# Turning twelve blocks of rows by the DMA, as two planes of 16-bit halves, in a decoder layer on one core

## The chip, the cores and the metric

The kernel runs on one core of a Trainium2 chip. The metric is the device time of one execution in microseconds (us), the median of several runs. Beside it stands one execution taken by the hardware profiler, with a record for nearly every instruction and every DMA.

The engines, as the profile names them: PE multiplies matrices (PEld loads its weights), DVE is the vector engine, ACT the scalar engine, POOL the general one, and SP issues most of the DMAs. A DMA issued by an engine stands in that engine's own queue, in order with its other instructions: the profile calls them SPq and ACTq.

## The reference

One decoder layer, batch 1, 256 tokens, width 2048, all in float32. The part that matters here, with the weights' names:

```python
merged = sigmoid(g_a) * (ret_out @ w_proj_ret) + sigmoid(g_b) * (rnn_out @ w_proj_rnn)
h = h + merged @ w_mix_out
hn = rmsnorm(h, norm_xa_w)
h = h + memory_cross_attention(hn, mem_n, xa_w_q, xa_w_k, xa_w_v, xa_w_o)
hn = rmsnorm(h, norm_ffn_w)
h = h + conv_gated_ffn(hn, ffn_w_up, ffn_conv_w, ffn_conv_b, ffn_w_down)
```

`ret_out` comes from an eight-head retention, `rnn_out` from a gated linear recurrence; both, and the gates, are projections of the normalised input by `w_in`. What counts for the change is that `merged` and the two later values of `h` are each a 256 x 2048 matrix that the kernel makes with tokens on the partitions, and that the next product needs with features on the partitions.

## The kernel before

**The products.** Every weight matrix is read once, in chunks of 512 x 512 (KC = 4 row tiles of 128, 1 MB each), in the order of a list `plan`. `prefetch` (L182) issues the chunk's load on SP into `raw` (three buffers), then splits it into a high part `hi`, rounded to fp32r (a cast on ACT, L214), and a low part `lo` = raw - hi (DVE, L215); there are six buffers of each, two for a chunk. The other operand is split likewise, so that a product is three matmuls: high by high, low by high, high by low.

`gemm_n` (L283) makes a block of 256 tokens x 512 columns with tokens on the partitions, in four chunks of 24 matmuls when the inner size is 2048. `gemm_t` (L246) makes the block with features on the partitions, in four chunks of 32 matmuls. Both take their chunks from `chunks` (L229). It splits two chunks ahead (AHEAD), counts the chunks in `step`, and after each chunk runs what is due in the list `pending`. `later(n, fn)` (L225) puts a piece of work there that is to be issued n + 1 chunks on. So the side work (turning, softmax, recurrence) stands between the matmuls of later chunks. A scheduler then orders each engine's instructions: of those that are ready, the one that was written first.

**The operand by feature.** The operand of a product is a list of tiles, each holding two feature tiles of 128 for all 256 tokens, high half in columns 0 to 255 and low half in 256 to 511. `split_pair` (L323, ACT L330 and DVE L331) makes one with a common factor, `split_cols` (L349, ACT L353 and DVE L354) one with a factor for each feature (the norm's weight).

**The turns.** `transposed` (L303) turns rows on PE: for each 256 columns of a 512-column block, four 128 x 128 transposes against an identity matrix (`ident`, in `cid`) into one PSUM tile `sm` (L309). Three places use it for blocks of 512 columns that DVE has just finished:

- merged rows: `gated` (L679) makes gate times product for a block b; for the second gate DVE finishes the block (L686) and adds the other branch's (L698). `turn_merged` (L691) turns it. Its four blocks (b = 0 to 3) feed the product with `w_mix_out`.
- residual rows after the mixers, and after the attention: `residual` (L707) runs `gemm_n` with `w_mix_out` or `xa_w_o`, adds the block to the residual rows `hrow[b]` (DVE, L714), has ACT square them for the norm (L730), and puts two calls of `turn` (L720) on the list, one chunk apart, 256 columns each. The four blocks after the mixers become `h1s`, first read by the product with `xa_w_q`, after one of four chunks with `xa_w_k`. Those after the attention become `h2s`, read by the first product with `ffn_w_up`, which follows at once.

The first chunk of the product that follows reads tiles 0 and 1 of its list, the fourth tiles 6 and 7. So the last block (b = 3) of the merged rows has three chunks from its product's end until it is read, and so has the last block of `h2s`.

**Buffers and loads.** The tiles called `big` are 4 KB per partition and come from a pool of 27. The residual's own rows (`x`) and the memory tokens are loaded on SP between the third and the fourth product stage (L703, L704: eight loads of 512 KB), and squares of the memory rows (`rms`, L429, 16 instructions of ACT over the whole kernel, eight of them here) follow in the product with `w_mix_out` at b = 1.

PE also turns the retention's heads (`finish_head`, 32 transposes) and the attention's probabilities (16, L783).

Of the kernel before, what the change touches and what calls it, by code (L numbers as in the profile page):

```python
# [9 lines left out]
F32 = mybir.dt.float32  # L10
F32R = mybir.dt.float32r
I32 = mybir.dt.int32
AF = mybir.ActivationFunctionType
ALU = mybir.AluOpType
AX = mybir.AxisListType

P = 128
D = 2048
S = 256
# [8 lines left out]
BW = 512  # L28
# [36 lines left out]
def hybrid_layer(  # L65
# [25 lines left out]
    act, dve, pe, pool, sp = nc.scalar, nc.vector, nc.tensor, nc.gpsimd, nc.sync  # L91
# [11 lines left out]
    def nm(s):  # L103
        count[0] += 1
        return f"{s}_{count[0]}"

    def big(shape, dt=F32, s="b"):
        return bp.tile(shape, dt, tag="big", name=nm(s))
# [4 lines left out]
    def acc():  # L113
        return pm.tile([P, 2, BW], F32, tag="acc", name=nm("acc"))

    def small(shape=(P, 2, S)):
        return px.tile(list(shape), F32, tag="sm", name=nm("sm"))
# [24 lines left out]
    early = sp_.tile([P, 1], F32, tag="pt3", bufs=2, name="early")  # L142
    act.activation(early, ones[:, 0:1], AF.Identity, scale=ones[:, 1:2])
    warm = px.tile([P, 2, S], F32, tag="sm", name="warm")
# [80 lines left out]
    def later(n, fn):  # L225

        pending.append((step[0] + n + 1, fn))

    def chunks(nk, w, row, c):  # L229

        w_, row_, nk_, c_ = plan[gemms[0]]
        assert (row_, nk_, c_) == (row, nk, c) and w_.tensor is w.tensor, (gemms[0], row, nk, c)
        gemms[0] += 1
        for k in range(0, nk, KC):
            prefetch(1)
            (r_, c_), parts = ahead.pop(0)
            assert (r_, c_) == (row + k * P, c)
            prefetch(AHEAD)
            yield k, parts
            step[0] += 1  # L240
            due = [p for p in pending if p[0] <= step[0]]
            pending[:] = [p for p in pending if p[0] > step[0]]
            for _, fn in due:
                fn()

    def gemm_t(w, row, st, nk, col):  # L246

        accs = [acc(), acc()]
        first = gemms[0] == 0
        phase = 0  # L250
        for k0, parts in chunks(nk, w, row, col):
            last = k0 + KC >= nk
            tiles = [(kk, j) for j in range(2) for kk in range(KC)]
            if first and k0 == 0:
                runs = [[(t, pr, kk, j) for t in (0, 1)] for pr in range(2) for kk in range(KC) for j in range(2)]
            elif last:
                runs = [[(t, pr, kk, j) for kk, j in tiles] for pr in range(2) for t in (1 - pr, pr)]
            else:
                runs = [[(t, pr, kk, j) for pr in range(2) for kk, j in tiles] for t in (phase, 1 - phase)]
                phase = 1 - phase  # L260
            for i, run in enumerate(runs):
                for t, pr, kk, j in run:
                    k = k0 + kk
                    sx = st[k // 2][:, k % 2, :]
                    part = parts[kk // KH][t][:, kk % KH, (2 * pr + j) * P : (2 * pr + j + 1) * P]
                    a = accs[pr][:, j, :]
                    if t == 1:
                        a, sx = a[:, S:BW], sx[:, 0:S]
                    pe.matmul(  # L269
                        a, part, sx, start=k == 0 and t == 0, stop=k == nk - 1 and t == 0, skip_group_check=True  # L270
                    )
                if i + 1 == len(runs) // 2 and not last:
                    st[(k0 + KC) // 2 + 1]
        return accs

# [27 lines left out]
    def transposed(rows):  # L303

        for k in range(0, rows.shape[2], 2 * P):
            t = small()
            for j in range(2):
                for tt in range(2):
                    pe.transpose(  # L309
                        t[:, j, tt * P : (tt + 1) * P], rows[:, tt, k + j * P : k + (j + 1) * P], ident  # L310
                    )
            yield t

    def joined(a, s="j"):

        c = tmp("c")
        o = tmp(s)
        with tc.high_priority(URGENT):
            act.copy(c, a[:, :, S:BW])  # L319
            dve.tensor_tensor(out=o, in0=a[:, :, 0:S], in1=c, op=ALU.add)  # L320
        return o

    def split_pair(src, scale=None):  # L323

        t = big([P, 2, BW], F32R, s="s")
        if scale is None:
            act.copy(t[:, :, 0:S], src)
            dve.tensor_tensor(out=t[:, :, S:BW], in0=src, in1=t[:, :, 0:S].bitcast(F32), op=ALU.subtract)
        else:
            act.mul(t[:, :, 0:S], src, scale)  # L330
            dve.scalar_tensor_tensor(  # L331
                out=t[:, :, S:BW], in0=src, scalar=scale, in1=t[:, :, 0:S].bitcast(F32),
                op0=ALU.mult, op1=ALU.subtract,
            )
        return t
# [13 lines left out]
    def split_cols(src, wcol):  # L349

        t = big([P, 2, BW], F32R, s="s")
        for j in range(2):
            act.activation(t[:, j, 0:S], src[:, j, :], AF.Identity, scale=wcol(j))  # L353
            dve.scalar_tensor_tensor(  # L354
                out=t[:, j, S:BW], in0=src[:, j, :], scalar=wcol(j), in1=t[:, j, 0:S].bitcast(F32),
                op0=ALU.mult, op1=ALU.subtract,
            )
        return t
# [60 lines left out]

    posi = big([P, S], I32, s="posi")  # L420
    sp.dma_start(out=posi, in_=positions[0].partition_broadcast(P))

    def rms(rows, pin=False):

        ss = sp_.tile([P, 2, 4], F32, tag="ss0", name=nm("ss"))
        for c in range(4):
            for tt in range(2):
                junk = tp.tile([P, BW], F32, tag="tmp", name=nm("junk"))
                i = act.activation(junk, rows[c][:, tt, :], AF.Square, accum_out=ss[:, tt, c : c + 1])  # L429
                if pin:  # L430
# [27 lines left out]
    def tables():  # L458
# [9 lines left out]
        dve.tensor_scalar(out=red, in0=red, scalar1=3.1415925, scalar2=-3.1415925, op0=ALU.min, op1=ALU.max)  # L468
        act.activation(sin, red, AF.Sin)
        dve.scalar_tensor_tensor(out=ang, in0=red, scalar=-1.0, in1=red, op0=ALU.mult, op1=ALU.max)  # L470
        dve.tensor_scalar(out=ang, in0=ang, scalar1=-1.0, scalar2=float(np.pi / 2), op0=ALU.mult, op1=ALU.add)
        act.activation(cos, ang, AF.Sin)
        dve.scalar_tensor_tensor(out=sin, in0=sin, scalar=sign, in1=rsb, op0=ALU.mult, op1=ALU.mult)
# [84 lines left out]
    for g in range(2):  # L558
        dec = big([P, 4, S], s="dec")
        vs, turned = [], []  # L560
        for b, o in enumerate((O_Q, O_K)):
            a = qjoin if g == b == 0 else [joined(t, "q") for t in gemm_t(w0, 0, xs, NT, o + g * BW)]
            if b == 0:
                sp.dma_start(
                    out=dec,
                    in_=consts[:, C_DEC + g * 4 * S : C_DEC + (g + 1) * 4 * S].rearrange("p (h s) -> p h s", s=S),
# [9 lines left out]
        for b in range(2):  # L576
            a = gemm_n(w0, 0, xs, NT, O_G + g * 1024 + b * BW)
            t = big([P, 2, BW], s="gate")
            for tt in range(2):
                act.activation(t[:, tt, :], a[:, tt, :], AF.Tanh, scale=half_rs0[:, tt : tt + 1])  # L580
            dve.scalar_tensor_tensor(out=t, in0=t, scalar=1.0, in1=a, op0=ALU.add, op1=ALU.mult)
# [67 lines left out]
    for b in range(4):  # L649
# [4 lines left out]
        for pr, a in enumerate(gemm_t(w0, 0, xs, NT, O_XR + b * BW)):  # L654
            z = scaled(a, "xz")
            for j in range(2):
                t = 4 * b + 2 * pr + j
                y = xr[:, 2 * pr + j, :]
                act.activation(y, z[:, j, :], AF.Identity, scale=p_cw(3, t), bias=p_cb(t))
                for s in range(1, 4):  # L660
                    dve.scalar_tensor_tensor(
                        out=y[:, s:S], in0=z[:, j, 0 : S - s], scalar=p_cw(3 - s, t), in1=y[:, s:S],
# [3 lines left out]
        for pr, a in enumerate(gemm_t(w0, 0, xs, NT, O_YR + b * BW)):  # L666
# [7 lines left out]
                out=gl[:, 2 * pr : 2 * pr + 2, :], in0=th, scalar=1.0, in1=y, op0=ALU.add, op1=ALU.mult  # L674
# [13 lines left out]

    merged = []

    def turn_merged(m, pr):  # L691
        for t in transposed(m[:, :, pr * S : (pr + 1) * S]):
            merged.append(split_pair(t, 0.5))

    mb = [gated(O_GB, w_proj_rnn[0], rnn, b, big([P, 2, BW], s="mb")) for b in range(4)]
    for b in range(4):
        m = gated(O_GA, w_proj_ret[0], ret, b, big([P, 2, BW], s="m"))
        dve.tensor_add(m, m, mb[b])  # L698
        for pr in range(2):
            later(pr, lambda m=m, pr=pr: turn_merged(m, pr))  # L700


    hrow = [load_rows(x, c) for c in range(4)]  # L703
# [3 lines left out]
    def residual(w, st, out, wcol, steps=None):  # L707

        ss = sp_.tile([P, 2, 4], F32, tag="ss0", name=nm("ss"))
        for b in range(4):  # L710
            if steps:
                steps(b)
            h = hrow[b]
            dve.tensor_add(h, h, gemm_n(w, 0, st, NT, b * BW))  # L714
            squares(h, ss, b)
            for pr in range(2):
                later(pr, lambda b=b, pr=pr: turn(b, pr, out, wcol))
        return ss

    def turn(b, pr, out, wcol):  # L720
        for t in transposed(hrow[b][:, :, pr * S : (pr + 1) * S]):
            out.append(split_cols(t, lambda j: wcol(4 * b + 2 * pr + j)))

    def squares(y, ss, i):
        for tt in range(2):
# [166 lines left out]
    for part, nb_ in enumerate(FF_PARTS):  # L892
# [13 lines left out]
        if final:  # L906
            wfin = []
            for i in range(2):
                t = big([P, 2, BW], s="wf")
                sp.dma_start(  # L910
                    out=t.rearrange("p a n -> p (a n)"),
                    in_=final_norm_w[i * 1024 : (i + 1) * 1024].partition_broadcast(P),
# [40 lines left out]
```

## Time and profile before

| | |
|---|---|
| runs shown | 2049.11, 2049.55, 2050.26 us; median 2049.55 |
| profiled execution, its own time | 2048.89 us |
| its span, first to last instruction | 2047.1 us |
| granted PE clock | 0.999 of full speed |
| PE, DVE, ACT busy | 2035.0, 1309.3, 1045.3 us |
| transposes of the three places | 96: 32 of `m`, 64 of `nat` |
| DMA | 392.25 MB, mean 192 GB/s |

A stage is found by the lines that work in it. In microseconds from the span's start: the second gate's four blocks end at about 836, the product with `w_mix_out` runs from there to about 923, the attention's four products fill the time to about 1220, the product with `xa_w_o` lies at about 1221 to 1308, and the feed-forward part from 1308 to the end.

How to read the profile's lines: "x64" counts instructions; "270/272/273" is the shortest, median and longest duration in ns; "out<-in" names the tiles that an instruction writes and reads; what stands behind a bar or in brackets is the idle time of the engine before the instruction, and what ended it. Matmuls overlap in PE's pipeline, so that a duration is longer than the step from one start to the next. The chain of waits follows back, from the last instruction, what released each piece of work, and gives each piece the time by which it moved the end.

### The profile page before, as it was taken

To read this page: it belongs to the slowest core of one execution; us is meant where nothing else is said; L and a number is where in the kernel's file an instruction comes from. 1 tells how busy PE (TensorE), PEld (TensorE's weight loads), DVE (VectorE), ACT (ScalarE), POOL (GpSimd) and SP (SyncE) were. 2 spreads that over 40 slices of the span, in tenths; PEclk is the share of its full clock that TensorE was granted. 3 is DMA by queue.
4 is the path that set the end of the run, shared out by engine and by line. 5 is a ranking of instruction groups with operands and counts; after the bars stand their busy time and mean duration, and the time that the engine had idled before them with its cause. 6 is when DMAs were issued, how large, how long until landed. Compare 5 with 4: busy or idle time off the path is not lost.

```text
span 2047.1 us, 26196 instructions
## 1 busy us (share of the span) xinstructions
PE 2035.0 (99%) x10508; PEld 1746.4 (85%) x10508; DVE 1309.3 (64%) x1630; ACT 1045.3 (51%) x1357; POOL 7.7 (0%) x12
## 2 busy tenths in 40 slices
PE   9999999999999999999999999999999999999998
PEld 7888888888888888888888888888888888888887
DVE  6858758888444544566555555577764777656774
ACT  6545447677434444555444544455543555435553
POOL 0000000000000000000000000000000000000000
PEclk9999999999999999999999999999999999999999
DMA  9664554555655555766555555555555555655563
GB/s 327 210 211 152 199 191 160 175 178 180 209 187 196 192 185 190 261 210 211 176 178 176 174 173 176 179 180 198 193 185 205 184 188 185 202 189 182 189 216 114
DMA packets 200682, 392.25 MB, mean 192 GB/s; under 512 B 7024, under 2 KB 11760, under 8 KB 200560
## 3 DMA queue, kind: packets, MB, share of 16 engines
q1 hardware_dynamic: 199040, 387.95, 55.7%
q10 hardware_dynamic: 1520, 2.63, 0.4%
q8 instruction: 82, 1.34, 0.3%
q14 instruction: 40, 0.33, 0.0%
HBM read 388.46 MB, written 2.10 MB: 191 GB/s over the span
## 4 chain that ended last, share of the span: by engine, by line
PE 79%; DVE 0%; ACT 0%; issue 0%; POOLq 0%; DVEq 0%
PE acc L269 35%; PE acc L280 14%; PE acc L281 14%; PE acc L279 14%; PE sm L297 1%; PE sm L309 1%; PE sm L623 0%; DVE xr L640 0%; PE sm L783 0%; ACT hi L214 0%; ACT nat L878 0%; DVE lo L215 0%; ACT c L319 0%; PE sm L380 0%; ACT s L330 0%
## 5 line engine op out<-in xcount | busy, mean ns | idle before, releaser
L215 DVE TENSOR_TENSOR lo<-raw,hi 128x1024 fp32r<-128x1024 f32 (+1 forms) x713 | 860.3, 1222 | 608.4 <-ACT hi L214 562.4
L214 ACT CAST hi<-raw 128x1024 fp32r<-128x1024 f32 x711 | 736.2, 1052 | 718.3 <-PE acc L280 455.0
L269 PE MATMUL acc<-s,hi 128*128 128x512 f32 x2688 | 639.0, 391 | 2.5 <-ACT hi L214 1.9
L279 PE MATMUL acc<-hi,s 128*128 128x512 f32 (+1 forms) x1528 | 591.9, 387 | 0.0
L281 PE MATMUL acc<-lo,s 128*128 128x512 f32 (+1 forms) x1528 | 590.1, 386 | 0.0
L280 PE MATMUL acc<-hi,s 128*128 128x512 f32 (+1 forms) x1528 | 590.0, 386 | 0.0
L269 PEld LDWEIGHTS acc<-s,hi 128*128 128x128 f32 x2688 | 496.5, 188 | 101.7 <-ACT hi L214 2.7
L269 PEld LDWEIGHTS acc<-s,lo 128*128 128x128 f32 x2688 | 342.7, 191 | 11.8 <-DVE lo L215 1.1
L269 PE MATMUL acc<-s,lo 128*128 128x256 f32 x2688 | 350.4, 283 | 0.5 <-DVE lo L215 0.5
L281 PEld LDWEIGHTS acc<-lo,s 128*128 128x128 f32 x1528 | 287.1, 188 | 57.9
L280 PEld LDWEIGHTS acc<-hi,s 128*128 128x128 f32 x1528 | 287.2, 188 | 57.1 <-DVE s L331 0.4
L279 PEld LDWEIGHTS acc<-hi,s 128*128 128x128 f32 x1528 | 287.2, 188 | 56.6
L319 ACT COPY c<-acc 128x512 f32<-128x512 f32 x84 | 48.6, 581 | 111.8 <-PE acc L269 111.8
L320 DVE TENSOR_TENSOR uz<-acc,c 128x512 f32<-128x512 f32 x44 | 30.3, 688 | 27.4 <-ACT c L319 27.4
L835 DVE SCALAR_TENSOR_TENSOR fg<-uz,pf,fg 128x255 f32<-128x255 f32 (+1 forms) x88 | 39.2, 479 | 0.0
L835 DVE SCALAR_TENSOR_TENSOR fv<-uz,pf,fv 128x255 f32<-128x255 f32 (+1 forms) x88 | 38.4, 480 | 0.0
L353 ACT ACTIVATE s<-sm,pb 128x256 fp32r<-128x256 f32 x48 | 21.9, 471 | 17.7 <-DVE s L354 16.7
L443 DVE TENSOR_TENSOR uz<-uz,rsb 128x512 f32<-128x512 f32 x44 | 30.3, 689 | 0.7
L330 ACT ACTIVATE s<-fo 128x512 fp32r<-128x512 f32 x22 | 13.9, 632 | 26.7 <-DVE fo L904 26.7
L833 ACT ACTIVATE fv<-uz,pf 128x256 f32<-128x256 f32 x44 | 25.3, 600 | 2.5 <-DVE uz L443 2.5
L354 DVE SCALAR_TENSOR_TENSOR s<-sm,pb,s 128x256 fp32r<-128x256 f32 x48 | 22.4, 481 | 5.1 <-ACT s L353 5.1
L833 ACT ACTIVATE fg<-uz,pf 128x256 f32<-128x256 f32 x44 | 25.3, 599 | 0.0
(167 smaller groups left out, 731.0 us busy)
## 6 DMA issues: line engine op xcount, KB each, us to landing
raw<-in_w_in SPq DMA_DIRECT2D x109, 1024.0 KB, 5.0
raw<-in_ffn_w_up SPq DMA_DIRECT2D x88, 1024.0 KB, 4.9
raw<-in_ffn_w_down SPq DMA_DIRECT2D x44, 1024.0 KB, 5.1
raw<-in_w_proj_rnn SPq DMA_DIRECT2D x16, 1024.0 KB, 5.1
raw<-in_w_proj_ret SPq DMA_DIRECT2D x16, 1024.0 KB, 5.1
raw<-in_w_mix_out SPq DMA_DIRECT2D x16, 1024.0 KB, 5.1
raw<-in_xa_w_k SPq DMA_DIRECT2D x16, 1024.0 KB, 5.1
raw<-in_xa_w_q SPq DMA_DIRECT2D x16, 1024.0 KB, 5.1
```

The costliest lines, as they stand in the source:

```text
L214: act.copy(hi[:, ds], raw[:, cs, :])
L215: dve.tensor_tensor(out=lo[:, ds], in0=raw[:, cs, :], in1=hi[:, ds].bitcast(F32), op=ALU.subtract)
L269: pe.matmul(a, part, sx, start=k == 0 and t == 0, stop=k == nk - 1 and t == 0, skip_group_check=True)
L279: pe.matmul(o, h, hi, start=start, stop=False)
L280: pe.matmul(o, l, hi, start=False, stop=False)
L281: pe.matmul(o, h, lo, start=False, stop=stop)
L319: act.copy(c, a[:, :, S:BW])
L320: dve.tensor_tensor(out=o, in0=a[:, :, 0:S], in1=c, op=ALU.add)
L354: dve.scalar_tensor_tensor(out=t[:, j, S:BW], in0=src[:, j, :], scalar=wcol(j), in1=t[:, j, 0:S].bitcast(F32), op0=ALU.mult, op1=ALU.subtract,
L443: dve.tensor_tensor(out=z, in0=z, in1=rsb2, op=ALU.mult)
L833: act.activation(y, z[:, j, :], AF.Identity, scale=pf[:, 2, t : t + 1], bias=pf[:, 3, t : t + 1])
L835: dve.scalar_tensor_tensor(out=y[:, s:S], in0=z[:, j, 0 : S - s], scalar=pf[:, 2 - s, t : t + 1], in1=y[:, s:S], op0=ALU.mult, op1=ALU.add,)
```

## The change

The three places no longer turn on PE. A new function `by_dma(rows, then)` takes a block of rows (128 partitions, two token tiles, 512 columns of float32) and

- has ACT copy the block, seen as 16-bit words, into a tile `planes`, the low halves of the words apart from the high halves: two copies of 128 x 1024 elements;
- issues two transposing DMAs on ACT's queue, one for each token tile, from `planes` to a tile `turned_` (128 x 1024 words of 16 bits each, 256 KB);
- puts `join` on the list, two chunks on: two copies by ACT that weave the halves to float32 in a tile `f` with features on the partitions, and then the splits as before, which now read `f` in SBUF and not `sm` in PSUM.

`planes`, `turned_` and `f` are `big` tiles. `turn_merged` and `turn` only split; the 512 columns that came in two calls a chunk apart come in one. In `gemm_t` the line that touched the next tile of the operand ahead of time now does so only for the two operands that are loaded by feature (`Pairs`), since a plain list need not hold that tile yet.

```diff
+U16 = mybir.dt.uint16
...
-                if i + 1 == len(runs) // 2 and not last:
+                if i + 1 == len(runs) // 2 and not last and isinstance(st, Pairs):
                     st[(k0 + KC) // 2 + 1]
...
+    def by_dma(rows, then):
+
+
+        planes = big([P, 2, 2, BW], U16, s="pl")
+        turned_ = big([P, 2, 4, S], U16, s="pt")
+        words = rows.bitcast(U16).rearrange("p t (n h) -> p h t n", h=2)
+        for h in range(2):
+            act.copy(planes[:, :, h, :], words[:, h])
+        for tt in range(2):
+            act.dma_start_transpose(
+                out=turned_.rearrange("p h f s -> p (h f) s")[:, :, tt * P : (tt + 1) * P],
+                in_=planes[:, tt].rearrange("p h n -> p (h n)"),
+            )
+
+        def join():
+            f = big([P, 4, S], s="f")
+            halves_ = f.bitcast(U16).rearrange("p f (s h) -> p h f s", h=2)
+            for h in range(2):
+                act.copy(halves_[:, h], turned_[:, h])
+            then(f)
+
+        later(1, join)
...
-    def turn_merged(m, pr):
-        for t in transposed(m[:, :, pr * S : (pr + 1) * S]):
-            merged.append(split_pair(t, 0.5))
+    def turn_merged(f):
+        for pr in range(2):
+            merged.append(split_pair(f[:, 2 * pr : 2 * pr + 2, :], 0.5))
...
         dve.tensor_add(m, m, mb[b])
-        for pr in range(2):
-            later(pr, lambda m=m, pr=pr: turn_merged(m, pr))
+        by_dma(m, turn_merged)
...
             squares(h, ss, b)
-            for pr in range(2):
-                later(pr, lambda b=b, pr=pr: turn(b, pr, out, wcol))
+            by_dma(hrow[b], lambda f, b=b: turn(f, b, out, wcol))
         return ss
 
-    def turn(b, pr, out, wcol):
-        for t in transposed(hrow[b][:, :, pr * S : (pr + 1) * S]):
-            out.append(split_cols(t, lambda j: wcol(4 * b + 2 * pr + j)))
+    def turn(f, b, out, wcol):
+        for pr in range(2):
+            out.append(split_cols(f[:, 2 * pr : 2 * pr + 2, :], lambda j: wcol(4 * b + 2 * pr + j)))
```

## The prediction

> **What bounds the kernel now.** First the page's busy times:
>
> ```profile
> span 2047.1 us, 26196 instructions
> ## 1 busy us (share of the span) xinstructions
> PE 2035.0 (99%) x10508; PEld 1746.4 (85%) x10508; DVE 1309.3 (64%) x1630; ACT 1045.3 (51%) x1357; POOL 7.7 (0%) x12
> ```
>
> PE leaves 12 us of 2047. Busy time proves little for pipelined matmuls, so I read the chain of waits next, here where the residual after the mixers is turned for the last time:
>
> ```profile
> 927.42 5.54 PE acc L269 x32
> 932.96 0.44 PE sm L309 x4
> 933.40 5.61 PE acc L269 x32
> 939.01 0.44 PE sm L309 x4
> 939.45 38.97 PE acc L269 x224
> ```
>
> The columns are start, length and work. A chunk of 32 matmuls moves the end by 5.54 to 5.61 us, a group of four transposes by 0.44, with no wait between: PE's instructions themselves are the limit, and each one taken out moves the end. Then the busy times by stretch (us, then PE, PEld, DVE, ACT, POOL busy with counts, clock, DMA share, GB/s), for the products with w_mix_out and xa_w_o and for the start of the first:
>
> ```profile
> 843.00:931.00 88.00, 88.00 (x405) 72.82 (x404) 50.65 (x61) 50.16 (x84) 0.70 (x1) 1.00 0.69 235
> 1228.00:1322.00 94.00, 94.00 (x449) 78.56 (x448) 51.76 (x56) 47.20 (x66) 0.70 (x1) 1.00 0.53 179
> ...
> 838.00:843.00 5.00, 5.00 (x26) 4.15 (x25) 4.06 (x4) 2.11 (x2) 0.00 (x0) 1.00 1.01 354
> 843.00:848.00 5.00, 5.00 (x26) 4.15 (x25) 1.65 (x2) 1.87 (x2) 0.00 (x0) 1.00 1.05 392
> 848.00:853.00 5.00, 5.00 (x24) 4.10 (x23) 2.57 (x4) 1.23 (x3) 0.00 (x0) 1.00 1.05 385
> ```
>
> PE is never idle there, ACT is idle for 38 and 47 us, and from 838 to 853 the DMA engines are full: the eight loads of x and mem (512 KB each). Last, what ACT's weight casts wait for (total us, times, longest):
>
> ```profile
> ACT hi L214 <- PE acc L280: 455.0, 314, 3.5
> ```
>
> They wait for PE to free a buffer. With six buffers of hi, two to a chunk, a cast is made for the third chunk on, and its first half may run about two chunks (10.9 us) before it is needed. That is ACT's slack.
>
> **What goes.** 96 transposes, 24 groups of four:
>
> ```profile
> L309 PE MATMUL sm<-cid,nat x64: 270/272/273, 864.0 to 1320.0; 128*128 128x128 f32 x64
> ...
> L309 PE MATMUL sm<-cid,m x32: 270/272/273, 707.8 to 847.5; 128*128 128x128 f32 x32
> ```
>
> The duration of 272 ns is pipeline length. What one group displaces is 0.44 us by the chain. By the spacing it is 0.46: the groups at 864.19 and 870.11 stand 5.92 us apart, where 24 matmuls at their step of 0.2273 us take 5.46. I take 0.45: 24 x 0.45 = 10.8 us, all of it on the path. The splits read SBUF now: ACT's 128x256 form took 503 ns from xt against 471 from sm, so 48 x 0.03 = 1.5 us more on ACT, inside its idle time. What is late next is nothing while ACT, DVE and the weight stream keep up: a chunk needs 2.1 us of casts on ACT and 2.45 us of subtractions on DVE in 5.46 us, and the weights land 5.0 us after issue with three buffers.
>
> **What comes.** For each of 12 blocks:
>
> - Four ACT copies of 128x1024. No row shows 16-bit words at a stride; the nearest is the weight cast of the same count, 1052 ns. Bounds: half of that and twice that. I take 1.05, so 4.2 us a block and 50 us in all.
> - Two transposing DMAs issued by ACT. No row shows one. A plain DMA holds ACT's queue for 0.38 to 0.51 us; at most it holds it until the data have landed, for which 5.0 us (a weight chunk) is the row. I take the nearest, 0.5.
> - Their landing, from the second issue: 256 KB to HBM landed in 2.7 us (median of `out`) on idle DMA engines; 512 KB in the full stretch took 6.5 to 11.8 us, median 9.6. So 2.7 to 11. I take 2.7 where the engines have room, and 6.5 for the block that falls in the full stretch.
> - 6 MB more for the DMA engines, of 392: nothing, at a share of 0.55.
>
> Ten blocks have over a gemm of time before they are read, or three chunks with other tiles read first; two are read three chunks later.
>
> Merged rows, block 3. The product with w_mix_out starts at 841.46 - 5.47 = 836.0, so its fourth chunk, which reads tiles 6 and 7, starts at 836.0 + 3 x 5.46 = 852.4 without transposes. DVE's sum (L698) starts at 838.96 and ends at 840.2. ACT then makes the planes, with a weight cast among them (3.1 us): 843.3. Issues: 844.3. Landing at 6.5: 850.8. Joins (2.1): 852.9. First split (0.63 ACT, 0.68 DVE): 854.2. So 1.8 us late; between nothing (landing 2.7) and 6.4 (landing 11.1).
>
> h2s, block 3. The first feed-forward product starts at 1308.26, its fourth chunk at 1308.26 + 3 x 5.55 = 1324.9. ACT ends the squares (L730) at 1311.5, planes 1313.6, issues 1314.6, landing 1317.3 (DMA share 0.68 there); two casts and the joins until 1321.4, four splits of 0.48 and DVE's last until 1323.8. In time by 1.1 us. Before, the second of its two groups ran on PE at 1319.81, ready at 1323.7: the change takes the slack of a moved wait, not more.
>
> Casts behind all this. The worst place is ACT from 860.67, where two squares (1.25 us) are followed by eight squares of mem (8 x 0.617 = 4.9). Now planes and issues (3.1) come between. From about 859.8: 869.1, then a cast until 870.1 and DVE's lo until 871.3, needed at 857.8 + 16.4 = 874.2. In time by 2.9 us; at two issues of 2 us each nothing is left, and what exceeds that is paid by PE.
>
> **Sum** against the profiled execution: 2048.89 - 10.8 + 1.8 = 2039.9. The median shown is 0.66 higher, so 2040.5. The joins wait for the DMA on ACT; queued behind them are the casts, and behind those lo and PE, with the slack above. SP's queue waits only for raw buffers that lo frees, and POOL's 12 instructions for neither.
>
> **The rivals.**
>
> 1. *The hand-over eats it.* With landings at the upper row (11.1) merged block 3 is 6.4 us late and h2s block 3, 11.1 - 2.7 - 1.1 = 7.3. The gain of 10.8 is gone at a sum of the two of 10.8, that is from landings of about 9.7 us; at 11.1 the time is 2049.55 - 10.8 + 13.7 = 2052.5. For it: the full stretch. Against: the DMA engines idle half the time at 1308 to 1323, and a scheduler that may let PE take other ready work.
> 2. *ACT becomes the bound (slower).* The mechanism: ACT works in order, and each transposing DMA holds it for X. In the product with w_mix_out ACT has 88 - 50.2 = 37.8 us free for four blocks, 9.45 a block, less 4.2 for copies: 5.25. In the product with xa_w_o it has (94 - 47.2) / 4 - 4.2 = 7.5. Above that each block delays the casts and so PE: 4 (2X - 5.25) + 4 (2X - 7.5). It decides from X = 3.9, where this equals 10.8. At X = 5.0 it is 29 us, and the time 2049.55 - 10.8 + 29 = 2068. Against: the plain issue's 0.4 to 0.5 us. For: no row bounds X below the landing time, and a wait at the join adds to it.
> 3. *The DMA transposes slowly.* A 512 KB load on ACT's own queue landed in 10.4 us (median of nat<-in_x). If each transpose took as long and the second began after the first, 21 us together, the hand-overs would be 21 - 4.7 = 16 us late (merged, whose landing must come within 4.7 us of 844.3 to be in time) and 21 - 3.8 = 17 (h2s): 2049.55 - 10.8 + 33 = 2072. Against: those loads were twice the size and ran beside the first weights, and a 256 KB DMA took 2.7 us. The Trainium skill (VectorE: DVE Perf Modes, The three transpose paths) speaks for it: it sets 1309 ns by the DMA crossbar against 390 ns on TensorE for one 128 x 128 turn, and advises TensorE when PSUM will do; eight such turns in each DMA, one after another, would be an estimate of 21 us a block. The trace already differs on TensorE's side, 0.11 us of PE's time for a turn (0.45 / 4); at 390 ns the 96 would give back 37 us. The Trainium skill (Advanced Engine Details and Errata, X-Bar Transpose (TRN2)) says the opposite, that these DMAs are as fast as ordinary ones, by which the sum above stands; no run here shows which.
>
> That the transposes stay is excluded: turn and turn_merged no longer call `transposed`.
>
> **Chances.** Measurements of this kernel tell from no change what exceeds about 0.2% (4.1 us). Forecast, 2037.5 to 2045.4: 0.64. Rival 1, around no change: 0.14. Rival 2: 0.16. Rival 3: 0.06. So faster 0.64, same 0.14, slower 0.22. The low end is the sum without any stall (2038.7) less a microsecond; the high end has to take in rival 1 and the beginning of rival 2, X about 4.4 (2058), to leave out no more than 0.2.
>
> **What would show it.** Right: no `sm<-cid,m` or `sm<-cid,nat` group, PE still without idle time in the stretches above, the step from chunk to chunk at 5.46, and the only new PE wait at the fourth chunk after 836, for `s` written at L330 or L331. Rival 1: a wait there or in the first feed-forward product of over 4 us. Rival 2: PE waiting for hi (L214) all through both products, and ACT idle behind its own issues or at the joins. Rival 3: landings of `pt` over 10 us. The forecast is wrong if 16-bit copies take twice 1.05 us, which alone takes 4.2 us a block, or if issues exceed 2 us.

## The result, and the profile after

The changed kernel takes 2058.43 us (median of four runs, 2058.18 to 2061.13), against 2049.86 for the kernel before in the same measurement: 1.0044 times as long, 95% interval 1.0031 to 1.0056. The prediction was 2040.5, faster. The profiled execution of the changed kernel is the run of 2061.13 us, so that in its trace the loss is 12.2 us against the profiled 2048.89, and not 8.6. Lines are those of the changed kernel from here on, where a name in front says nothing else: L215 is the cast and L216 the subtraction of a weight, L322 and L333 the two pairs of copies, L324 the transposing DMA, L377 and L378 `split_cols`, L737 the residual sum, L752 its squares.

The head of its page:

```profile
span 2059.0 us, 26063 instructions
## 1 busy us (share of the span) xinstructions
PE 2030.8 (99%) x10412; PEld 1740.4 (85%) x10412; DVE 1306.4 (63%) x1630; ACT 1090.9 (53%) x1405; POOL 7.7 (0%) x12
```

The 96 transposes are gone (10412 matmuls, 10508 before), but PE is idle for 2059.0 - 2030.8 = 28.2 us where it was 12.1. And it is busy only 4.2 us less. Two runs further down have the same 10412 matmuls without the longest wait (the issue on SP's queue, and no DMA at all); in both PE is busy for 2025.1 us, 9.9 less than before. So there are 16.1 us of new waits here and 5.7 us of slower matmuls: 16.1 + 5.7 - 9.9 = 11.9, the difference of the two spans. What PE waited for (total us, times, longest):

```profile
PE acc L270 <- ACT s L377: 10.5, 1, 10.5
PE acc L270 <- ACT hi L215: 3.7, 2, 2.5
PE sm L404 <- DVE diag L403: 2.7, 2, 2.3
PE acc L280 <- ACT hi L215: 1.1, 1, 1.1
```

One wait is two thirds of it. Where it lies is seen in the busy times by stretch (us, PE, PEld, DVE, ACT, POOL busy, clock, DMA share, GB/s):

```profile
880.00:900.00 20.00, 16.93 (x67) 13.08 (x67) 11.66 (x16) 14.51 (x23) 0.70 (x1) 0.91 0.59 168
...
935.00:960.00 25.00, 14.48 (x75) 12.87 (x75) 13.77 (x23) 16.18 (x30) 0.69 (x1) 0.80 0.72 233
...
1225.00:1315.00 90.00, 90.00 (x410) 74.97 (x410) 48.64 (x50) 57.82 (x75) 0.00 (x0) 1.00 0.65 201
...
947.00:951.00 4.00, 3.71 (x17) 3.72 (x18) 3.31 (x7) 4.00 (x10) 0.00 (x0) 0.50 0.55 102
```

Nearly all of it (15.8 us between 843 and 960) is in the product with w_mix_out and at the start of the next, with xa_w_k. The product with xa_w_o (1225 to 1315) has the same copies and DMAs, and PE without an idle moment. The granted clock, 1.00 before, is 0.50 in the four microseconds after the long wait. Now ACT around that wait (start, length, work, idle time before it and what ended it):

```profile
938.53 1.97 ACT L322 COPY pl<-nat 128x1024 uint16<-128x1024 uint16 x2
940.41 1.04 ACT L215 CAST hi<-raw 128x1024 fp32r<-128x1024 f32 x1
940.53 6.15 ACTq L324 DMA_TRANSPOSE pt<-pl  x2
946.73 1.71 ACT L377 ACTIVATE s<-xt,pb 128x256 fp32r<-128x256 f32 x4 [5.28 <-issue]
948.34 1.03 ACT L215 CAST hi<-raw 128x1024 fp32r<-128x1024 f32 x1
```

The split at 946.73 makes part of the memory operand (`xt`) from which PE goes on at 947.29. It needs nothing from the transposing DMAs. It stands behind them in ACT's queue, and they hold the queue for 6.15 us: ACT is idle for 5.28 us, ended by `issue`, its own next instruction. That is half of PE's wait, which began at 936.77, before this pair was issued. The other half is ACT's order ahead of the pair: the chain of waits goes back from the split over a cast, the copies at 938.53, the squares and DVE's sum of the block at 936.04. The pair of the last block after the attention held it far more shortly:

```profile
1326.21 2.67 ACTq L324 DMA_TRANSPOSE pt<-pl  x2
```

All 24 issues and their landings (shortest, median, longest; ns, then us), and the copies by form (count, busy us, mean ns, idle before):

```profile
L324 ACTq DMA_TRANSPOSE pt<-pl x24: 1248/1377/6458, 711.3 to 1327.5; - x24
DMA to landing us min/median/max: 3.3/5.3/11.5
```

```profile
L333 ACT COPY f<-pt 128x1024 uint16<-128x1024 uint16 x24 | 30.7, 1345 | 13.3 <-DMA pt<-pl 13.1
...
L322 ACT COPY pl<-nat 128x1024 uint16<-128x1024 uint16 x16 | 15.8, 1037 | 0.0
```

By pair, from the timeline of ACT's queue, the holds are 3.40, 2.67, 3.37 and 7.90 us (merged rows 0 to 3), 4.46, 5.57, 4.77 and 6.15 (after the mixers), 2.90, 2.85, 2.66 and 2.67 (after the attention): 49.4 us in all. Where the issues were seen one by one, the first of a pair took 1.25 to 2.03 us; in the pairs of over 4 us the long part was the second's.

SP's queue was stopped as well. Its loads of mem waited for the landing of a transposing DMA of merged block 3, and two weight loads behind them, which the kernel before issued at 843.60 and 849.53, went out at 854.44 and 854.95. First SP's wait (total us, times, longest), then a piece of the chain of waits (start, length, work), a weight chunk that landed at 866.13:

```profile
SPq L126 <- DMA pt<-pl: 9.8, 1, 9.8
```

```profile
854.95 11.17 DMA raw<-in_w_mix_out
```

The load does not need the turned words. In the program as it is built, the two share a completion counter, and the later DMA waits until the earlier one has landed.

### The profile page after: what moved, and what is told of

The parts are those of the page before. It is cut to its first block, busy times and chain, and to the rows that moved or that the text cites. A ratio compares the mean times of both kernels' runs of the same rounds, so it can differ in the third digit from the quotient of the medians.

```text
span 2059.0 us, 26063 instructions
## 1 busy us (share of the span) xinstructions
PE 2030.8 (99%) x10412; PEld 1740.4 (85%) x10412; DVE 1306.4 (63%) x1630; ACT 1090.9 (53%) x1405; POOL 7.7 (0%) x12
## 4 chain that ended last, share of the span: by engine, by line
PE 74%; ACT 2%; DVE 1%; ACTq 1%; DMA 1%; issue 1%; POOLq 0%; SPq 0%; DVEq 0%
PE acc L270 35%; PE acc L281 12%; PE acc L280 12%; PE acc L282 12%; PE sm L298 1%; ACTq L324 1%; DVE lo L216 1%; ACT hi L215 1%; DMA raw<-in_w_mix_out 1%; ACT pl L322 0%; PE sm L647 0%; DMA pt<-pl 0%; ACT f L333 0%; ACT junk L453 0%; ACT junk L752 0%
## 5 line engine op out<-in xcount | busy, mean ns | idle before, releaser
L216 DVE TENSOR_TENSOR lo<-raw,hi 128x1024 fp32r<-128x1024 f32 (+1 forms) x713 | 857.4, 1221 | 599.5 <-ACT hi L215 556.2
L215 ACT CAST hi<-raw 128x1024 fp32r<-128x1024 f32 x711 | 731.8, 1049 | 671.8 <-PE acc L281 402.6
L270 PEld LDWEIGHTS acc<-s,lo 128*128 128x128 f32 x2688 | 344.8, 192 | 22.6 <-ACT s L377 10.7
L270 PE MATMUL acc<-s,lo 128*128 128x256 f32 x2688 | 352.5, 285 | 11.0 <-ACT s L377 10.5
L333 ACT COPY f<-pt 128x1024 uint16<-128x1024 uint16 x24 | 30.7, 1345 | 13.3 <-DMA pt<-pl 13.1
L354 ACT ACTIVATE s<-fo 128x512 fp32r<-128x512 f32 x22 | 13.9, 631 | 27.0 <-DVE fo L926 27.0
L752 ACT ACTIVATE junk<-nat 128x512 f32<-128x512 f32 x22 | 13.7, 625 | 12.5 <-DVE nat L737 9.3
```

Source lines behind the costliest of these rows:

```text
L215: act.copy(hi[:, ds], raw[:, cs, :])
L216: dve.tensor_tensor(out=lo[:, ds], in0=raw[:, cs, :], in1=hi[:, ds].bitcast(F32), op=ALU.subtract)
L270: pe.matmul(a, part, sx, start=k == 0 and t == 0, stop=k == nk - 1 and t == 0, skip_group_check=True)
L333: act.copy(halves_[:, h], turned_[:, h])
```

## The experiments

**Theory H** (hold): a transposing DMA holds the queue of the engine that issues it, the longer the more the DMA engines have before them, and what stands behind it on ACT is late. **Rivals: C**, the four ACT copies of a block are too much for ACT; **L**, the turned words land too late, and what waits for them costs the time.

**The issue moved to SP's queue.**

```diff
-            act.dma_start_transpose(
+            sp.dma_start_transpose(
```

> The 24 transposing DMAs are issued on SP's queue and not on ACT's; the rest is the changed kernel. Theory H (hold): a transposing DMA holds the queue that issues it, 1.3 us where the DMA engines have room and up to 6.5 us where they are full, and on ACT the weight casts and the memory splits stand behind it. Then ACT's idle time at `issue` in the product with w_mix_out goes, the 10.5 us wait for the memory splits falls to under 3 us, and the time is 2040 to 2046 unless SP's loads, now held in ACT's place, come late. Theory C (copies): ACT is overloaded by the four copies of each block, 4.7 us; moving the issue changes nothing, 2055 to 2059. Theory L (landing): the turned words come too late in the full stretch; nothing changes either, 2055 to 2059.

Measured: 2040.82 us, 0.9957 of before (0.994 to 0.9973). It is 17.6 us less than the changed kernel, and C falls: the copies are still there. Issues and landings, and PE's waits (the one for the memory splits, 10.5 us, is not among them any more):

```profile
L324 SPq DMA_TRANSPOSE pt<-pl x24: 1243/1308/3144, 710.6 to 1307.0; - x24
DMA to landing us min/median/max: 3.1/3.8/5.6
```

```profile
PE acc L270 <- ACT hi L215: 3.0, 1, 3.0
...
PE acc L270 <- ACT s L377: 1.0, 1, 1.0
```

SP is held as well (up to 3.1 us), but behind it stand only loads. The words also land earlier (median 3.8 us, not 5.3), and SP's loads of mem no longer wait for them, so this run alone does not part H from L.

**No DMA at all.** The transposing DMAs are left out, and the joins read the planes, so the rows are not turned.

```diff
-        turned_ = big([P, 2, 4, S], U16, s="pt")
+        turned_ = planes
...
-        for tt in range(2):
-            act.dma_start_transpose(...)
...
```

> Leaves out the turning: no transposing DMA, the joins read the planes, so the product's operands are the rows not turned; the four ACT copies of each block and the splits stay. Theory H: the stalls go, PE saves its 96 transposes, 2038 to 2041. Theory C: the copies alone overload ACT in the product with w_mix_out, and at least half of the 16 us of new PE idle time stays: 2046 to 2056. Theory L: as H, 2038 to 2041.

Measured: 2040.10 us, 0.995 (0.9935 to 0.9965). With the copies, taking out the transposes is worth 9.8 us of the 10.8, so that the copies alone cost 1 us at the most. PE's longest wait is one of 2.3 us for a cast, of which the kernel before has one of 1.9 us.

**A plain DMA in the transposing one's place.** The rows are again not turned; the same words go to a second tile by two plain DMAs of 256 KB a block on ACT's queue, and the joins wait for them.

```diff
...
-            act.dma_start_transpose(...)
+            act.dma_start(
+                out=turned_[:, tt].rearrange("p h n -> p (h n)"),
+                in_=planes[:, tt].rearrange("p h n -> p (h n)"),
+            )
...
```

> Leaves out the turning, but moves the same 256 KB twice a block from the planes to a second tile by plain DMAs on ACT's queue, for which the joins wait as before. Theory H, if it is the transposing DMA that holds the queue: issues of 0.4 to 0.5 us and 2038 to 2043. Theory L: the copies land as late as the turned words did (5 to 11 us in the full stretch), and the time stays at 2052 to 2059. If any DMA on ACT's queue is held when the DMA engines are full, issues of several us show in the product with w_mix_out, and 2050 to 2059.

Measured: 2047.72 us, 0.9989 (0.998 to 0.9998), above H's range and below L's.

```profile
L324 ACTq DMA_DIRECT2D pt<-pl x24: 472/560/1621, 710.0 to 1312.5; - x24
DMA to landing us min/median/max: 2.3/3.8/8.0
```

```profile
PE acc L270 <- ACT s L377: 4.8, 2, 4.4
```

A plain DMA hardly holds the queue (0.56 us). But the time is 7.6 us above that without any DMA, and landings delay others here in two places: the joins waited 12.6 us for them, five times, with casts and splits behind them on ACT; and SP's load of mem waited 5.4 us for one, with a weight load behind it. So a share of L is real; how the 7.6 us divide between the two places is not shown. That the transposing DMA costs 10.7 us more than the plain one (2058.43 - 2047.72), with the same bytes, is its hold and its later landing together.

**Which blocks.** `by_dma` is used for some of the blocks, and the others turn on PE as before, here for the attention alone:

```diff
...
-            by_dma(hrow[b], lambda f, b=b: turn(f, b, out, wcol))
+            if b in (() if out is h1s else (0, 1, 2, 3)):
+                by_dma(hrow[b], lambda f, b=b: turn(f, b, out, wcol))
+            else:
+                turn_pe(hrow[b], lambda t, pr, b=b: out.append(split_cols(t, lambda j: wcol(4 * b + 2 * pr + j))))
```

> Only the four blocks of the residual after the attention (xa_w_o) go by the DMA; the merged rows and the residual after the mixers turn on PE as before. Theory H: there the DMA engines have room, the holds are 1.3 to 1.6 us, no PE wait comes, and 32 transposes are saved: 8 x 0.45 = 3.6 us, so 2046.3. Theory C: four copies of 4.7 us a block cost as much here as in the product with w_mix_out, so 2050 to 2053. Theory L: in time here, 2046.3.

> Seven of the twelve blocks go by the DMA on ACT's queue: merged rows 0 to 2 and the four after the attention. The other five (merged rows 3 and the residual after the mixers), which fall where SP's loads of x and mem and the memory tiles are under way, turn on PE. Theory H: holds of 1.2 to 2 us each, no new PE wait, 7 x 0.9 = 6.3 us saved: 2043.6, between 2042.5 and 2045. If every block cost what the twelve cost on average (8.6 / 12 = 0.7 us), 2054.9.

> The other half: only merged rows 3 and the four blocks of the residual after the mixers go by the DMA on ACT's queue. Theory H: five blocks save 4.5 us, and the loss of 19.4 us (8.6 measured plus 10.8 saved) is all theirs: 2049.9 - 4.5 + 19.4 = 2064.8, between 2060 and 2068, with PE waiting for the memory splits behind the last pair. If the loss were spread evenly over twelve blocks, 2053.4.

> Only the four blocks of the residual after the mixers go by the DMA on ACT's queue; merged rows turn on PE, so nothing of the change comes before the first of them. Theory H: the four holds of 4 to 6 us are enough: 3.6 us saved, 15 to 20 lost, 2061 to 2066. If the delay starts with merged rows 3 (hold 7.9 us, weights late) and is only carried on, the holds here shrink and the time is 2047 to 2052.

> Only the last block of the merged rows goes by the DMA on ACT's queue, in the stretch where x and mem are loaded; the other eleven turn on PE. Theory H: a hold of 5 to 8 us, casts late, 0.9 us saved and up to 5 lost: 2049 to 2054. The hand-over that the prediction priced at 1.8 us (nothing to 6.4) would by itself give 2049.9 - 0.9 + 1.8 = 2050.8.

| blocks by the DMA on ACT's queue | us | ratio to before, 95% |
|---|---|---|
| after the attention (4) | 2046.14 | 0.9981 (0.9972 to 0.9991) |
| these and merged rows 0 to 2 (7) | 2043.46 | 0.9968 (0.9957 to 0.998) |
| merged rows 3 and after the mixers (5) | 2063.97 | 1.0067 (1.0052 to 1.0082) |
| after the mixers alone (4) | 2056.90 | 1.0032 (1.0021 to 1.0044) |
| merged rows 3 alone (1) | 2052.42 | 1.0014 (1.0004 to 1.0024) |

Seven blocks gain 0.9 us each, as the prediction priced a block; five lose 13.9 us, and the two halves add up to 7.4, near the 8.6 measured for all twelve. The two crowded parts alone lose 6.9 and 2.6 and together 13.9, more than their sum. In each run where merged block 3 goes by the DMA on ACT's queue, SP stands for 9.5 to 9.8 us at its load of mem, with weight loads behind it; with the blocks after the mixers alone it stands for 0.6 us. That this delay makes the later ones worse is likely, but no run shows it by itself. For the blocks after the mixers the truth lay between H's range and the alternative. Their holds, with PE's largest wait:

```profile
L324 ACTq DMA_TRANSPOSE pt<-pl x8: 1248/1756/4892, 865.9 to 935.2; - x8
```

```profile
PE acc L270 <- ACT s L377: 8.7, 1, 8.7
```

**The crowd brought to the roomy place.** In the kernel with the attention's four blocks by the DMA, three loads of 512 KB that nobody reads are issued on SP beside each pair.

```diff
             squares(h, ss, b)
+            if out is not h1s:
+                for c in range(3):
+                    g = big([P, 2, BW], s="cr")
+                    dve.tensor_copy(g[:, 0, 0:2], h[:, 0, 0:2])
+                    load_rows(mem, c, t=g)
```

> The kernel in which only the four blocks after the attention go by the DMA (2046.1), with three unneeded loads of 512 KB on SP's queue put beside each pair of transposing DMAs. Theory H, with the DMA engines' backlog as what sets the hold: the second DMA of a pair holds ACT's queue 3 to 6 us in place of 1.3 to 1.6, the casts behind it are late, and the time rises, to 2048 to 2060. If the hold in the product with w_mix_out comes from something else (ACT's own load, the squares of the memory rows), the holds stay at 1.3 to 1.7 us and the time at 2046 to 2047.5.

> All twelve blocks turn on PE, and the twelve unneeded loads of 512 KB stand after the attention as before. Theory H: the loads alone delay nothing that PE waits for, 2049.5 to 2051.5. If the loads themselves make the weights late, 2055 to 2064, and the rise by 13.6 us with the four transposed blocks says nothing on the hold.

> The four blocks after the attention by the DMA, the twelve unneeded loads beside them, but the transposing DMAs issued on SP's queue. Theory H: SP is held as ACT was (3 to 6 us), but behind it stand only loads that have a chunk and more of room; ACT's casts run on, and the time is 2046 to 2050 in place of 2059.7. If the late landing costs and not the hold (landings 8.5 to 9.6 us there), the wait of 8 us for the splits of the last block stays: 2054 to 2060.

Measured: 2059.70 us with the transposing DMAs on ACT (1.0046, 1.0029 to 1.0062), 2050.39 with the loads and all turns on PE (1.0003, 0.9994 to 1.0012), 2052.81 with the DMAs on SP (1.0014, 1.0005 to 1.0023). On ACT, without the loads, then with them:

```profile
L324 ACTq DMA_TRANSPOSE pt<-pl x8: 1248/1444/2742, 1245.3 to 1311.8; - x8
```

```profile
L324 ACTq DMA_TRANSPOSE pt<-pl x8: 1321/3034/5714, 1247.5 to 1321.7; - x8
DMA to landing us min/median/max: 8.5/9.1/9.6
```

```profile
PE acc L270 <- ACT s L377: 8.0, 1, 8.0
```

The loads alone cost nothing that can be told. With them, the same four blocks lose 13.6 us (2059.70 - 2046.14), and a pair holds ACT's queue for 6.1 to 7.1 us in place of 2.9 to 4.0: loads put beside the pairs lengthen the hold in this stage too, without the squares of mem. (The medians above lie between the first issue of a pair, short in both runs, and the second.) The issue from SP takes back 6.9 us of it. The rest goes with L: there the words landed after 5.9 to 9.9 us, and PE waited 4.7 us for the splits of the last block, which are needed three chunks on. H's range for that run (to 2050) was missed for this.

**The pair taken apart.** The blocks after the mixers alone, with the second DMA of a pair queued behind the third chunk's cast.

```diff
...
+        def second():
+            with tc.issue_after(last_cast[0]):
+                issue(1)
+
+        issue(0)
+        later(1, second)
...
-        later(1, join)
+        later(2, join)
```

> As the kernel in which only the residual after the mixers goes by the DMA on ACT's queue (2056.9), but the second transposing DMA of each pair is issued about a chunk (5.4 us) after the first, behind the casts of the third chunk on, and the join a chunk later. Theory H, that the second waits on ACT until the first has drained: each of the eight then holds ACT 1.2 to 2 us, the wait for the memory splits goes, and the time is 2046.3 (3.6 us saved) to 2050. If a transposing DMA in that stretch holds the queue whatever stands before it, the holds stay at 4 to 6 us a pair and the time at 2054 to 2059. Theory C (copies) predicts no change either.

Measured: 2051.25 us (1.0006, 0.9997 to 1.0016), 5.7 us less than with the pair together and above H's range. The spacing did not come about: the second started 1.3 to 2.7 us after the first, and not 5.4. ACT's queue at the last block:

```profile
932.05 1.35 ACTq L325 DMA_TRANSPOSE pt<-pl  x1
933.45 0.51 ACT L385 ACTIVATE s<-xt,pb 128x256 fp32r<-128x256 f32 x1 [0.48 <-DMA xt<-in_mem_t]
933.86 4.37 ACTq L325 DMA_TRANSPOSE pt<-pl  x1
933.87 1.30 ACT L385 ACTIVATE s<-xt,pb 128x256 fp32r<-128x256 f32 x3
935.07 1.03 ACT L216 CAST hi<-raw 128x1024 fp32r<-128x1024 f32 x1
936.00 1.70 ACT L385 ACTIVATE s<-xt,pb 128x256 fp32r<-128x256 f32 x4
938.28 1.31 ACT L385 ACTIVATE s<-xt,pb 128x256 fp32r<-128x256 f32 x3 [0.58 <-issue]
```

The pair still takes 6.2 us from the first's start to the second's end. But eight memory splits and a cast now stand in the program between the two. The queue took up the second issue at 933.86, while most of them had still to run, and ACT ran seven splits and the cast beside it until 937.7; then it was idle for 0.58 us, where it was for 5.3 us with the pair together. So a held queue is not yet an idle ACT: what was queued ahead of the issue goes on, and for the same reason an issue placed later in the program started hardly later. PE's wait for a memory split is 1.9 us in place of 8.7. The run says nothing on whether a second DMA waits for the first, and much on what counts: not how long the queue is held, but what stands behind the hold.

## Why the prediction was wrong, step by step

**What goes: right.** Seven roomy blocks gained 6.6 us where 7 x 0.9 = 6.3 were priced, and without the DMAs all twelve gained 9.8 of 10.8. The Trainium skill's figures for one 128 x 128 turn (VectorE: DVE Perf Modes, The three transpose paths, for bf16: 390 ns on TensorE, 1309 ns by the DMA crossbar) were of use on neither side: a turn moved the end by 0.11 us on PE, and a DMA of eight such turns landed within 3.3 us of its issue in the best case, where eight at 1309 ns would be 10.5.

**Copies: near.** 1.04 us for the planes and 1.34 for the joins, 4.8 us a block in place of 4.2. They were hidden but for 1 us at the most.

**The issue: the step that failed.** "A plain DMA holds ACT's queue for 0.38 to 0.51 us; at most it holds it until the data have landed, for which 5.0 us (a weight chunk) is the row. I take the nearest, 0.5." Nearest in kind was not near in size: 24 issues held ACT for 49.4 us, not 12, and single ones for up to 6.46 us, beyond the upper bound too. The step "Casts behind all this" gave the point at which it hurts, two issues of 2 us each, and all five crowded pairs are past it (4.46 to 7.90 us). At that very place the pair holds seven of the eight squares of mem, and PE waits for what follows from them (L404, 2.3 us) and then for hi (1.1). The sentence that SP's queue waits only for raw buffers failed too: SP waited 9.8 us for the landing of a transposing DMA, which the sum had at nothing. With the issue on SP's queue, where ACT is not held and SP's loads of mem do not wait, the time is 2040.82, close to the 2040.5 of the prediction.

**Rival 2 had the mechanism and not the price.** It averaged: ACT's free time in the product, shared by four blocks, against 2X a block, deciding from X = 3.9. The four blocks after the mixers have 2X = 5.24 on average, just under the 5.25 that the formula allows, and yet lose. The term that was missing is the order behind the hold. At 940.53 the memory splits for the product that PE had already begun stood behind 6.15 us, in a wait of PE of 10.5 us. The prediction looked at the casts, which have two chunks of slack, and not at the splits of `xt`, which had none: even with the issue on SP's queue PE waited 1.0 us for them. That the result is the 2058 which the prediction names for X about 4.4 is chance; by the holds that were measured its formula gives no loss.

**A cost that no step had: the clock.** After the long wait the granted clock was 0.50 for some four microseconds and 0.89 for the next four, and it was 0.62 from 884 to 888 after the waits before 884:

```profile
884.00:888.00 4.00, 3.87 (x10) 2.29 (x10) 4.00 (x7) 4.00 (x8) 0.00 (x0) 0.62 0.00 0
```

By these shares of PE's busy time the three stretches make up an estimated 3.8 of the 5.7 us of slower matmuls; where the rest lies is not shown. The Trainium skill has the rule (TensorE: Matmul & The Clock Gate, Part 1): the clock is halved after an idle window of about 3.4 us and comes back after as much work. The long wait fits it; the trace's lower clock after waits of 2.3 and 1.1 us shows that less than one whole window of idle time in one piece can do.

**The hand-overs.** For merged block 3 the prediction took a landing of 6.5 us and a delay of 1.8. It landed after 10.7 to 11.5 us, at the upper end of 11, and the splits ended at 858.7. Yet PE lost only 0.43 us from 843 to 853 and nothing that the trace counts from 853 to 863. In the changed program's order the first 24 matmuls of the next block stand ahead of the fourth chunk of block 0: the scheduler had put other ready work there, which rival 1 allowed for. For h2s block 3 the hand-over was in time, as said.

**Rival 3: no.** Landings beyond 10 us came for one pair alone, in the full stretch. The Trainium skill's other sentence (Advanced Engine Details and Errata, X-Bar Transpose (TRN2)), that such DMAs are as fast as ordinary ones, holds roughly for the landing, 3.3 us at best against 2.7 for 256 KB of `out`. It does not hold for the issue, 1.25 us at the least against 0.38 to 0.51.

What stays open: how the hold depends on the two DMAs of a pair standing together, since the one run for it did not space them; whether it is the backlog of the DMA engines or SP's own issuing that lengthens it; and how the 17.6 us that the issue from SP took back divide between the hold, the earlier landing and SP's loads, which no longer wait. The plain DMA on ACT's queue, with hardly a hold, still lost 7.6, so it is not the hold alone.

## What to carry to other kernels

An issue is an instruction in its engine's queue, and its length has to be measured for the kind of DMA and the load of the DMA engines at that moment; put such issues on a queue behind which nothing urgent stands, here SP's (2040.82 us, against 2058.43 on ACT's). To price a hold, do not set an engine's free time against it on average: list what stands behind it and when each of these is needed, and list also what waits for its landing. A wait of PE costs more than its length when it is long enough for the clock to fall.

## What the runs showed of the hardware that was not expected

- A transposing DMA of 128 x 1024 16-bit words held the queue that issued it for at least 1.25 us, on ACT and on SP; the second of a pair held ACT for up to 6.46 us when SP's loads were under way. A plain DMA of the same 256 KB held it for 0.56 us at the median, 1.62 at most.
- ACT's queue took up an issue while ACT had still seven splits and a cast of a weight to run that stood ahead of it, and ACT ran them during the 4.37 us of the hold.
- ACT's copy of 1024 16-bit words per partition took 1.04 us where only the reading was at a stride of two, and 1.34 us where the writing was.
- After 10.5 us without a matmul the granted clock was 0.50 for the next 4 us, and 0.89 in the four after.
